# Attention heads: transposes three slots behind their scores, the output projection's first two channel tiles with the fourth pair last, and filling in slots without steps

## The chip, the cores and the metric

The kernel runs on one core of one Trainium2 chip. TensorE (PE) does the matrix products; its weight loads stand in a row of their own (PEld). VectorE (DVE), ScalarE (ACT) and GpSimd (POOL) do the elementwise work, and the queue of SyncE (SP) issues nearly all transfers. The metric is the device time of one execution in microseconds.

## The reference, cut to what matters

Two residual layers over 512 frames of 1024 channels, each followed by a gated MLP. The first layer mixes by pooling, the second by attention with 16 heads of 64 channels. The change lies in the second one alone.

```python
def chunk_attention(h, w_qkv, q_norm, k_norm, rel_table, w_o):
    qkv = h @ w_qkv
    q, k, v = jnp.split(qkv, 3, axis=-1)
    q = head_rmsnorm(q.reshape(B, S, N_HEADS, HEAD_DIM), q_norm)
    k = head_rmsnorm(k.reshape(B, S, N_HEADS, HEAD_DIM), k_norm)
    ...
    def one_chunk(c):          # 64 queries of chunk c, keys of this chunk and the 8 before it
        s = jnp.einsum('bqhd,bkhd->bhqk', qc, kb) * scale + bias[None]
        s = jnp.where(valid[None, None, None, :], s, -1e30)
        p = jax.nn.softmax(s, axis=-1)
        return jnp.einsum('bhqk,bkhd->bqhd', p, vb)
    ...
    return o @ w_o             # added to x
```

## The kernel before

Activations are kept with channels in the partitions: X[0..7] are eight tiles of 128 channels by 512 frames in float32. For accuracy a product is made of three matmuls (`mm3`, L121 to L125: high by high, high by low, low by high part), so every operand is split into a high and a low part (`split`, L94 to L103: ACT or POOL copies the high part, DVE or POOL subtracts it from the raw value for the low part).

`attention` (L917) first projects part of the queries and keys (`project(0)`) and all values, and then runs a loop over 64 **slots** (L1131): slot i holds the steps of tile i, where tile i is head i // 4 and frame block t = i % 4 of 128 frames. A head pair p is two heads, 128 channels. The steps of a slot, in the order in which PE gets them:

- `scores(h, t)` (L1049): two matmuls of up to 512 columns into a PSUM tile `sc`; DVE adds the bias and takes the row's extreme value (L1066), ACT takes the exponential (L1068), DVE the reciprocal (L1069), ACT scales by it (L1070) into the tile `sb`. The biases B of a head are loaded when its first tile comes (L1057, SP's queue).
- `channel_major(p, i)` (L1026) in the third and fourth slot of every eight: four PE transposes of the next pair's queries (i = 0) or keys (i = 1) into a PSUM tile `zt`. For the queries ACT makes the high part `zh` and DVE the low part `zl` (L108); for the keys ACT makes `zh` (L1036) and DVE two half tiles of the low part, `kl` (L1039).
- `turn(h, t)` (L1072): t + 1 PE transposes of `sb` into a PSUM tile `tp`, split by ACT and DVE into `pt..h` and `pt..l` (L102, L103). It comes LAG slots behind the tile's scores.
- `mix(h)` (L1081): eight matmuls, four with the high and four with the low part of the transposed probabilities, into a PSUM tile `oo`, LAGM slots behind the head's last turn; ACT copies one half (`ob`, L1095) and DVE adds the other (`o`, L1096).

When both heads of pair p are mixed, its sum is split into XS[p] and XS[8 + p], halves of the tiles `two` (L1150).

Between the steps `fill` (L1116) puts single matmuls of other products, evenly over the slots: the remaining three projections up to slot 35.5 (matmuls `qk`), then `outputs` (L1022), 144 matmuls `wo` of the output projection from slot 35.5 to slot 64 + FO with FO = LAG + 6. `output(ps_)` (L996) goes through the channel tiles d = 0..7; for each it adds the products with the pairs of `ps_` in a PSUM bank of tag P or Q and lets DVE add the bank to X[d]. `outputs` does this for pairs 0 to 3 and then for 4 and 5. Pairs 6 and 7 follow after the loop (`last_pairs`, L1156).

PE's order is the order in which the code is written (`manual_schedule`, L1113). DVE, ACT, POOL and SP are ordered by a scheduler when the program is built. Each engine works its instructions off in that order. Tiles `sc`, `zt`, `tp` and `oo` share the tag S with four PSUM banks; which of the four a tile gets is settled when the program is built, too, and its first matmul waits until the bank's last tile has been read.

Of the kernel before, what the change touches and what calls it, by code (L numbers as in the profile page):

```python
# [23 lines left out]
P = 128  # L24
S = 512
D = 1024
KD = D // P
# [16 lines left out]
BANKS = {"PQ": 2, "SS": 4}  # L44


LAG, LAGM = 2, 2
FE = (3.5, 19.5, 35.5)
FO = LAG + 6
CM = (2, 3)  # L50
# [22 lines left out]
def trunk(ctx: ExitStack, tc: tile.TileContext, xt, xT, cols, band, edge, poolw, gv, wout, wqk, wv, wo, rel, out):  # L73
    nc = tc.nc
# [7 lines left out]
    X = [act.tile([P, S], F32, name=f"X{k}") for k in range(KD)]  # L82
# [6 lines left out]
    def psum(tag, name, bufs=2):  # L89
        return ps.tile([P, S], F32, name=name, tag=tag, bufs=bufs)  # L90
# [19 lines left out]
    def load_split(src, n, name, pool=None, eng=None, tag=(None, None), eng_hi=None):  # L110

        raw = wp.tile([P, 1024], F32, name=f"{name}_r", tag="wr")
        if pool:
            hi, lo = (pool.tile([P, n], F32R, name=f"{name}_{c}", tag=t, bufs=2 if t == "as" else 1) for c, t in zip("hl", tag))
        else:
            hi, lo = (wp.tile([P, 1024], F32R, name=f"{name}_{c}", tag=f"w{c}", bufs=2) for c in "hl")
        nc.sync.dma_start(raw[:, :n] if len(src.shape) == 2 else raw.rearrange("p (a b) -> p a b", a=src.shape[1]), src)
        split(raw[:, :n], hi[:, :n], lo[:, :n], eng, eng_hi)
        return hi, lo

    def mm3(o, sh, sl, mh, ml, first, last, **how):  # L121

        yield nc.tensor.matmul(o, sh, mh, start=first, stop=False, **how)  # L123
        yield nc.tensor.matmul(o, sh, ml, start=False, stop=False, **how)  # L124
        yield nc.tensor.matmul(o, sl, mh, start=False, stop=last, **how)  # L125

    def run(steps):
        step = None
        for step in steps:
            pass  # L130
        return step
# [9 lines left out]
    def small(name, n, tag="nw"):  # L141
        return tmp.tile([P, n], F32, name=name, tag=f"{tag}{n}", bufs=4)
# [774 lines left out]
    def attention():  # L917
        XS = set2
# [74 lines left out]

            yield from products(ov, wv[half], f"wv{half}", evict=evict)

        def output(ps_, after=None):  # L996

            p0, p1 = ps_[0], ps_[-1] + 1
            n = (p1 - p0) * P
            nd = D // n  # L1000
            w = {}

            def load(d):
                eng = nc.gpsimd if p0 < 6 else None
                w[d] = load_split(wo[d:d + nd, :, p0 * P:p1 * P].rearrange("d p m -> p d m"), D, f"wo{d}_{p0}", eng=eng, eng_hi=eng)

            for d in range(KD):
                if d % nd == 0:
                    if d not in w:
                        load(d)  # L1010
                    hi, lo = w[d]
                o = psum("PQ"[d % 2], f"wo{d}_{p0}")
                for p in ps_:
                    s = slice(d % nd * n + (p - p0) * P, d % nd * n + (p - p0 + 1) * P)
                    yield from mm3(o, hi[:, s], lo[:, s], XS[p], XS[KD + p], p == p0, p == p1 - 1)
                nc.vector.tensor_add(X[d], o, X[d])
                if after:
                    after(d)
                    if d == 1:
                        load(nd)  # L1020

        def outputs():  # L1022
            yield from output(range(4))
            yield from output((4, 5))

        def channel_major(p, i):  # L1026
# [22 lines left out]
        def scores(h, t):  # L1049

            p, e = divmod(h, 2)
            q, k, kl = QK[p, 0][e], QK[p, 1][e], KL[p % 2][e]
            if t == 0:

                base = rdram[h, :]
                for r, n in ((0, S - HD), (HD, S)):
                    nc.sync.dma_start(BT[h % 2][r:r + HD, S - n:], bass.AP(tensor=base.tensor, offset=base.offset + HD, ap=[[1, HD], [1, n]]))  # L1057
            n = (t + 1) * P
            nw = max(n, 256)

            sc = psum("S", f"sc{h}_{t}", 4)
            nc.tensor.matmul(sc[:, :nw], q[:, t * P:n], k[:, :nw], start=True, stop=False)
            nc.tensor.matmul(sc[:, :nw], q[:, t * P:n], kl[:, :nw], start=False, stop=True)  # L1063
            SM[h, t] = s_ = big.tile([P, n], F32, name=f"sb{h}_{t}", tag=f"sb{t}")
            mx = tmp.tile([P, 3], F32, name=f"mx{h}_{t}", tag="mx", bufs=4)
            nc.vector.tensor_tensor_reduce(out=s_[:, :n], in0=sc[:, :n], in1=BT[h % 2][:, :n][:, ::-1], scale=1.0,  # L1066
                                           scalar=3e38, op0=OP.add, op1=OP.min, accum_out=mx[:, 0:1])
            nc.scalar.activation(s_[:, :n], s_[:, :n], AF.Exp, scale=-1.0, bias=mx[:, 0:1], accum_out=mx[:, 1:2])  # L1068
            nc.vector.reciprocal(mx[:, 2:3], mx[:, 1:2])  # L1069
            nc.scalar.activation(s_[:, :n], s_[:, :n], AF.Copy, scale=mx[:, 2:3])  # L1070
# [28 lines left out]
        rcol, r2, late = None, small("r2", TT), []  # L1099
# [13 lines left out]
        with tc.manual_schedule(engines={mybir.EngineType.PE}):  # L1113
            cur, done, kept = 0, 0, 0

            def fill(upto):  # L1116

                nonlocal cur, done
                while cur < len(fillers):
                    g, n, a, b = fillers[cur]  # L1120
                    due = n * (upto - a) / (b - a)
                    while done < min(due, n):
                        next(g)
                        done += 1
                    if upto < b:
                        return
                    run(g)
                    cur, done = cur + 1, 0

            fill(0)  # L1130
            for i in range(nb + LAG + LAGM):  # L1131
                steps = []
                if i < nb:
                    steps.append(lambda: scores(*tiles_[i]))
                if i % 8 in CM and i // 8 + 1 < NPAIR:
                    steps.append(lambda: channel_major(i // 8 + 1, CM.index(i % 8)))
                j = i - LAG
                if 0 <= j < nb:
                    steps.append(lambda: turn(*tiles_[j]))
                j2 = j - LAGM  # L1140
                if 0 <= j2 < nb and j2 % TT == TT - 1:
                    steps.append(lambda: mix(tiles_[j2][0]))
                for x, step in enumerate(steps):
                    step()
                    if late and x < 2:
                        late.pop(0)()
                    fill(i + (x + 1) / len(steps))

                while 8 * kept + 7 <= j2 and (cur == 3 or cur == 2 and done >= 24 * (kept // 2 + 1)):
                    split(O2[kept], XS[kept], XS[KD + kept])  # L1150
                    kept += 1
            fill(nb + FO)
# [37 lines left out]
    with tc.tile_pool(name="ba", bufs=1) as big:  # L1190
        rest = attention()
# [55 lines left out]
```

## Time and profile before

| what | value |
|---|---|
| times of three runs | 972.45, 971.93, 1357.0 us (median 972.45) |
| the profiled execution: its own time | 972.12 us |
| its span in the profile | 970.3 us |
| PE busy, share of the span | 961.6 us, 99% |
| PEld | 815.0 us, 84% |
| DVE | 809.6 us, 83% |
| ACT | 576.6 us, 59% |
| POOL | 102.9 us, 11% |
| PE's share of the chain that ended last | 94% |
| the 64 slots of the loop, first scores to last mix | 452 us to 607 us of the span |

The profiled execution's own time is 1.8 us above its span; the text compares with this execution. A row of the timeline reads: start, duration, engine, line, operation, output tile, input tiles, shapes, and how many instructions are merged in it; in brackets the engine's idle time before it and what ended it. Names leave buffer numbers out: `pt1l` is the low part of the transposed probabilities of odd heads, `two` any XS tile.

### The profile page before, as it was taken

How to read it: one execution, taken by the hardware profiler on the slowest of the kernel's cores; microseconds unless marked ns; L12 is line 12 of the kernel's file. 1: busy time of each engine (PE TensorE's matmuls, PEld its weight loads, DVE VectorE, ACT ScalarE, POOL GpSimd, SP SyncE). 2: the span in 40 equal slices, each digit the busy share in tenths (PEclk: the TensorE clock that was granted, in tenths of full speed). 3: DMA queues.
4: the chain of work that ended last, by engine and by line, in shares of the span. 5: the costliest groups of instructions: out<-in, count | busy, mean ns of one | idle time of the engine just before them, and what ended most of it. 6: DMA issues, size and time to landing. Idle time of an engine off the chain costs nothing.

```text
span 970.3 us, 13704 instructions
## 1 busy us (share of the span) xinstructions
PE 961.6 (99%) x4982; PEld 815.0 (84%) x4982; DVE 809.6 (83%) x1462; ACT 576.6 (59%) x990; POOL 102.9 (11%) x90
## 2 busy tenths in 40 slices
PE   8999999999999999999999999999999999999998
PEld 7788988888888888888888787888988888888886
DVE  8999999999899854442777888999999999989953
ACT  7665564655555544345898988646565565566531
POOL 2300000000000013204534532000000000000000
PEclk9999999999999999999999999999999999999999
DMA  9222332332323224232343341332233233332323
GB/s 342 77 93 71 114 113 75 120 120 92 105 76 120 78 84 147 94 121 91 111 115 107 97 118 55 101 108 80 94 114 104 87 120 108 104 103 77 116 79 109
DMA packets 37427, 102.82 MB, mean 106 GB/s; under 512 B 4432, under 2 KB 7904, under 8 KB 37360
## 3 DMA queue, kind: packets, MB, share of 16 engines
q1 hardware_dynamic: 37296, 101.90, 33.0%
q8 instruction: 39, 0.64, 0.3%
q14 instruction: 28, 0.23, 0.1%
q0 software_dynamic: 32, 0.04, 0.0%
q10 hardware_dynamic: 32, 0.00, 0.0%
HBM read 95.60 MB, written 2.14 MB: 101 GB/s over the span
## 4 chain that ended last, share of the span: by engine, by line
PE 94%; DVE 4%; ACT 2%; issue 0%; DMA 0%; DVEq 0%; ACTq 0%
PE st_m L610 11%; PE out L124 8%; PE out L123 8%; PE out L125 8%; PE st_m L612 6%; PE st_t L610 6%; PE gv L124 4%; PE gv L123 4%; PE gv L125 4%; PE qk L124 3%; PE qk L123 3%; PE qk L125 3%; PE st_t L612 3%; PE st_b L610 3%; PE tp L1078 2%; PE oo L1090 2%
## 5 line engine op out<-in xcount | busy, mean ns | idle before, releaser
L124 PE MATMUL out<-one,ow_h 128*128 128x512 f32 x224 | 87.9, 393 | 0.0
L123 PE MATMUL out<-one,ow_h 128*128 128x512 f32 x224 | 87.8, 392 | 0.0
L125 PE MATMUL out<-one,ow_l 128*128 128x512 f32 x224 | 87.8, 392 | 0.0
L833 DVE TENSOR_TENSOR X<-out,X 128x512 f32<-128x512 f32 (+1 forms) x65 | 44.1, 680 | 49.1 <-PE out L125 48.9
L409 ACT ACTIVATE ow_h<-wo_r 128x640 fp32r<-128x640 f32 (+1 forms) x64 | 50.4, 788 | 56.4 <-PE out L124 46.8
L610 PE MATMUL st_m<-two,g_h 128*128 128x512 f32 x240 | 75.1, 394 | 0.0
L610 PE MATMUL st_m<-h,g_h 128*128 128x512 f32 x240 | 74.0, 389 | 0.0
L410 DVE TENSOR_TENSOR ow_l<-wo_r,ow_h 128x640 fp32r<-128x640 f32 (+1 forms) x64 | 56.5, 883 | 2.5 <-ACT ow_h L409 2.5
L424 DVE SCALAR_TENSOR_TENSOR c<-a,col,c 128x511 f32<-128x511 f32 (+1 forms) x76 | 56.3, 743 | 0.0
L610 PEld LDWEIGHTS st_m<-h,g_h 128*128 128x128 f32 x240 | 45.1, 188 | 10.3
L612 PEld LDWEIGHTS st_m<-two,g_l 128*128 128x128 f32 x240 | 45.0, 188 | 9.5
L610 PEld LDWEIGHTS st_m<-two,g_h 128*128 128x128 f32 x240 | 44.0, 188 | 10.4 <-ACT w L619 0.8
L619 ACT ACTIVATE w<-st_m 128x512 f32<-128x512 f32 x30 | 17.9, 598 | 56.8 <-PE st_m L612 56.8
L125 PE MATMUL qk<-wqk_h,two 128*128 128x512 f32 x128 | 51.4, 402 | 0.0
L123 PE MATMUL qk<-wqk_h,two 128*128 128x512 f32 x128 | 50.8, 409 | 0.0
L124 PE MATMUL qk<-wqk_l,two 128*128 128x512 f32 x128 | 50.8, 397 | 0.0
L612 PE MATMUL st_m<-h,g_l 128*128 128x256 f32 x240 | 48.3, 283 | 0.0
L125 PEld LDWEIGHTS out<-one,ow_l 128*128 128x128 f32 x224 | 42.3, 189 | 6.3
L124 PEld LDWEIGHTS out<-one,ow_h 128*128 128x128 f32 x224 | 42.3, 189 | 6.3 <-DVE one L435 0.3
L612 PE MATMUL st_m<-two,g_l 128*128 128x256 f32 x240 | 47.6, 280 | 0.0
L123 PEld LDWEIGHTS out<-one,ow_h 128*128 128x128 f32 x224 | 42.3, 189 | 6.0
L1066 DVE CUSTOM_DVE_ANT_0 sb<-sc,B 128x128 f32<-128x128 f32 (+1 forms) x64 | 31.1, 486 | 18.9 <-PE sc L1063 18.1
(378 smaller groups left out, 2928.6 us busy)
## 6 DMA issues: line engine op xcount, KB each, us to landing
gv_r<-gv SPq DMA_DIRECT2D x86, 512.0 KB, 3.9
wo_r<-wout SPq DMA_DIRECT2D x32, 384.0 KB, 3.1
wo_r<-wout SPq DMA_DIRECT2D x32, 320.0 KB, 2.9
wqk_r<-wqk SPq DMA_DIRECT2D x16, 512.0 KB, 3.4
wv_r<-wv SPq DMA_DIRECT2D x8, 512.0 KB, 3.3
wo_r<-wo SPq DMA_DIRECT2D x8, 512.0 KB, 3.4
xt<-xt SPq DMA_DIRECT2D x4, 512.0 KB, 5.1
X<-xT SPq DMA_DIRECT2D x8, 256.0 KB, 7.4
```

The lines of the kernel that those rows point to most:

```text
L123: yield nc.tensor.matmul(o, sh, mh, start=first, stop=False, **how)
L124: yield nc.tensor.matmul(o, sh, ml, start=False, stop=False, **how)
L125: yield nc.tensor.matmul(o, sl, mh, start=False, stop=last, **how)
L409: nc.scalar.activation(hi[:, :n], raw[:, :n], AF.Copy)
L410: return hi, lo, lambda: nc.vector.tensor_sub(lo[:, :n], raw[:, :n], hi[:, :n].bitcast(F32))
L424: nc.vector.scalar_tensor_tensor(c[:, j:], a[:, :S - j], cw[2 - j], c[:, j:], op0=OP.mult, op1=OP.add)
L610: nc.tensor.matmul(o, hi[:, c], B[i, name], start=first and i == 0, stop=False, **how)
L612: nc.tensor.matmul(o[:, 0], lo[:, c], B[i, name][:, 0], start=False, stop=i == 3, **how)
L833: nc.vector.tensor_add(X[d][:, fs], o[:, fs], X[d][:, fs])
L1066: nc.vector.tensor_tensor_reduce(out=s_[:, :n], in0=sc[:, :n], in1=BT[h % 2][:, :n][:, ::-1], scale=1.0, scalar=3e38, op0=OP.add, op1=OP.m ...
L1078: nc.tensor.transpose(tp[:, j * P:(j + 1) * P], s_[:, j * P:(j + 1) * P], ident)
L1090: nc.tensor.matmul(oo[:, j * P:], V[j, h // 4][:, h % 4].rearrange("p a d -> p (a d)"), PT[e][c][:, 4 * j:3 * j + TT].rearrange("p t q -> ...
```

## The change

There are three edits in `attention`, and no instruction is added or removed on any engine.

1. LAG goes from 2 to 3: the turn of a tile comes one slot later, and with it the mix (LAGM stays 2). FO follows, so that the 144 fill matmuls of the output projection are spread to slot 73 instead of 72.
2. `output` gets an argument `late`. With late=2, which the call for pairs 0 to 3 uses, channel tiles 0 and 1 first take pairs 0, 1 and 2 each, and then pair 3 for the one and for the other; their banks in P and Q stay open together for that time.
3. A `fill(i + 1)` stands behind the steps of each slot. It issues something only in a slot without steps, which is slot 67, between the last turn (slot 66) and the last mix (slot 68).

```diff
-LAG, LAGM = 2, 2
+LAG, LAGM = 3, 2
...
-        def output(ps_, after=None):
+        def output(ps_, after=None, late=0):
...
+            o = {}
+
+            def product(d, p):
+                if d not in o:
+                    o[d] = psum("PQ"[d % 2], f"wo{d}_{p0}")
+                hi, lo = w[d // nd * nd]
+                s = slice(d % nd * n + (p - p0) * P, d % nd * n + (p - p0 + 1) * P)
+                yield from mm3(o[d], hi[:, s], lo[:, s], XS[p], XS[KD + p], p == p0, p == p1 - 1)
+
             for d in range(KD):
-                if d % nd == 0:
-                    if d not in w:
-                        load(d)
-                    hi, lo = w[d]
-                o = psum("PQ"[d % 2], f"wo{d}_{p0}")
+                if d % nd == 0 and d not in w:
+                    load(d)
+                if d < late:
+                    for p in ps_[:-1]:
+                        yield from product(d, p)
+                    if d + 1 < late:
+                        continue
+                    for e in range(late):
+                        yield from product(e, ps_[-1])
+                        nc.vector.tensor_add(X[e], o[e], X[e])
+                    continue
                 for p in ps_:
-                    s = slice(d % nd * n + (p - p0) * P, d % nd * n + (p - p0 + 1) * P)
-                    yield from mm3(o, hi[:, s], lo[:, s], XS[p], XS[KD + p], p == p0, p == p1 - 1)
-                nc.vector.tensor_add(X[d], o, X[d])
+                    yield from product(d, p)
+                nc.vector.tensor_add(X[d], o[d], X[d])
...
-            yield from output(range(4))
+            yield from output(range(4), late=2)
             yield from output((4, 5))
...
                     fill(i + (x + 1) / len(steps))
+                fill(i + 1)
```

What this does to the order of the engines is shown at three places. In the rows, a tile's name has its number in it: sc11_0 is head 11, block 0; oo9 head 9; zt6_1 the keys of pair 6; wo0_0 channel tile 0 of the call for pairs 0 to 3; two1 and two5 hold the high and low parts of pairs 2 and 3.

**PE around the mix of head 9.** Before, from the last of the key transposes of pair 6 to the mix:

```order
L1032 MATMUL zt6_1_5591<-ident_106,z3_3_5366 128x128
L124 MATMUL wo2_0_5548<-two5_101,wo2_0_h_5543 128x512
L1078 MATMUL tp10_1_5605<-ident_106,sb10_1_5526 128x128 x2
L125 MATMUL wo2_0_5548<-two1_97,wo2_0_l_5544 128x512
L1090 MATMUL oo9_5611<-pt1h_3627,one2_82 128x512
```

And now:

```order
L1046 MATMUL zt6_1_5587<-ident_106,z3_3_5362 128x128
L124 MATMUL wo2_0_5541<-two5_101,wo2_0_h_5536 128x512
L1092 MATMUL tp10_0_5601<-ident_106,sb10_0_5488 128x128
L125 MATMUL wo2_0_5541<-two1_97,wo2_0_l_5537 128x512
L1076 MATMUL sc11_0_5608<-z25_1_5355,z25_0_5315 128x256
L1077 MATMUL sc11_0_5608<-kl11_3632,z25_0_5315 128x256
L123 MATMUL wo2_0_5541<-two1_97,wo2_0_h_5536 128x512
L1092 MATMUL tp10_1_5618<-ident_106,sb10_1_5520 128x128 x2
L124 MATMUL wo2_0_5541<-two5_101,wo2_0_h_5536 128x512
L125 MATMUL wo2_0_5541<-two1_97,wo2_0_l_5537 128x512
L1104 MATMUL oo9_5625<-pt1h_3627,one2_82 128x512
```

The mix moved from the slot of the key transposes into the next slot, behind another turn and the next head's first scores. Its bank is another one as well: before, oo9 followed zt6_0 (the queries of pair 6) in its bank; now it follows zt6_1 (the keys). The same holds for oo11 with pair 7, and oo3 now follows the keys of pair 3; oo7 now follows sc9_0, the scores of its own slot.

**DVE at the same place.** Before:

```order
L1066 ISA sb10_3_5584,mx10_3_5585<-sc10_3_5581,B0_3637 128x512
L1066 ISA mx10_3_5585 128x1
L108 SCALAR_TENSOR_TENSOR zl6_0_5568<-zt6_0_5561,gq_109,zh6_0_5566 128x512
L103 TENSOR_TENSOR pt0l_3626<-tp10_0_5576,pt0h_3625 128x128
L1039 SCALAR_TENSOR_TENSOR kl00_3629<-zt6_1_5591,gq_109,zh6_1_5596 64x512
L1039 SCALAR_TENSOR_TENSOR kl01_3630<-zt6_1_5591,gq_109,zh6_1_5596 64x512
```

And now:

```order
L108 SCALAR_TENSOR_TENSOR zl6_0_5561<-zt6_0_5554,gq_109,zh6_0_5559 128x512
L1080 ISA sb10_3_5579,mx10_3_5580<-sc10_3_5576,B0_3637 128x512
L1080 ISA mx10_3_5580 128x1
L103 TENSOR_TENSOR pt1l_3628<-tp9_3_5568,pt1h_3627 128x4x128
L1053 SCALAR_TENSOR_TENSOR kl00_3629<-zt6_1_5587,gq_109,zh6_1_5592 64x512
L1053 SCALAR_TENSOR_TENSOR kl01_3630<-zt6_1_5587,gq_109,zh6_1_5592 64x512
L1080 ISA sb11_0_5611,mx11_0_5612<-sc11_0_5608,B1_3638 128x128
```

The low part of the queries now stands ahead of the scores of block 3, and the low part of head 9's last turn ahead of the two `kl`.

**PE at the first use of the fourth pair.** Before, in channel tile 0 (the last L125 of pair 2, then pair 3 from the second row on):

```order
L125 MATMUL wo0_0_5379<-two1_97,wo0_0_l_5375 128x512
L123 MATMUL wo0_0_5379<-two1_97,wo0_0_h_5374 128x512
L1062 MATMUL sc9_2_5452<-z24_1_5110,z24_0_5078 128x384
L1063 MATMUL sc9_2_5452<-kl01_3630,z24_0_5078 128x384
L124 MATMUL wo0_0_5379<-two5_101,wo0_0_h_5374 128x512
```

And now, behind the products of channel tile 1 with pair 2:

```order
L125 MATMUL wo1_0_5444<-two1_97,wo0_0_l_5366 128x512
L1076 MATMUL sc10_0_5485<-zh5_1_5354,zh5_0_5314 128x256
L1077 MATMUL sc10_0_5485<-kl10_3631,zh5_0_5314 128x256
L123 MATMUL wo0_0_5370<-two1_97,wo0_0_h_5365 128x512
L1092 MATMUL tp9_1_5495<-ident_106,sb9_1_5429 128x128 x2
L124 MATMUL wo0_0_5370<-two5_101,wo0_0_h_5365 128x512
```

Pair 3 is asked for nine matmuls of the filling later than before, among the scores of head 10 instead of those of head 9.

On SP's queue the loads of the biases of heads 10 and 11 changed places with their neighbours: those of head 11 now stand behind the first transfer of the queries of pair 6, and those of head 13 between the transfers of pair 7. POOL's order is the same as before.

## The prediction

> **What bounds the kernel now.** First the page: the span, the busy shares and the chain that ended last.
>
> ```profile
> span 970.3 us, 13704 instructions
> PE 961.6 (99%) x4982; PEld 815.0 (84%) x4982; DVE 809.6 (83%) x1462; ACT 576.6 (59%) x990; POOL 102.9 (11%) x90
> PE 94%; DVE 4%; ACT 2%; issue 0%; DMA 0%; DVEq 0%; ACTq 0%
> ```
>
> PE is the bound over the whole span. The change neither adds nor removes a matmul, so it can win only time in which PE stands still inside the loop, and lose by new waits there. The next view cuts the loop into windows; its columns are window, length and then the busy time of PE, PEld, DVE, ACT and POOL, the granted clock, the DMA share and GB/s.
>
> ```profile
> 452.00:544.00 92.00, 92.00 (x503) 77.62 (x502) 63.92 (x192) 79.32 (x189) 40.02 (x29) 1.00 0.37 109
> 544.00:553.00 9.00, 8.08 (x42) 5.87 (x42) 8.65 (x29) 7.55 (x23) 3.10 (x3) 1.00 0.45 129
> 553.00:585.00 32.00, 31.96 (x186) 26.75 (x186) 27.22 (x82) 28.45 (x76) 17.30 (x14) 1.00 0.37 98
> 585.00:600.00 15.00, 14.81 (x84) 12.11 (x83) 11.92 (x37) 13.06 (x35) 3.44 (x2) 1.00 0.29 87
> 600.00:607.00 7.00, 6.19 (x35) 4.95 (x34) 4.97 (x11) 5.06 (x9) 0.00 (x0) 1.00 0.01 2
> ```
>
> The clock is 1.00 throughout. PE is idle in none of the first 92 us (the projections fill them), and for 0.92 + 0.04 + 0.19 + 0.81 = 1.96 us behind. That undercounts, because a matmul's row is longer than its turn. The distance of two starts shows the turn:
>
> ```profile
> 602.96 0.60 PE L1078 MATMUL tp<-ident,sb 128*128 128x128 f32 x4
> 603.32 0.47 PE L123 MATMUL wo<-two,wo_h 128*128 128x512 f32 x1
> 603.63 0.39 PE L124 MATMUL wo<-two,wo_h 128*128 128x512 f32 x1
> 603.85 0.39 PE L125 MATMUL wo<-two,wo_l 128*128 128x512 f32 x1
> ```
>
> A matmul of 512 columns has a row of 0.39 but the next starts 0.22 to 0.23 behind it; four transposes take 0.36, and the matmul behind transposes 0.31. A distance above these is a wait, even where the rows touch. By starts I find the following waits between 544 and 607 us.
>
> The Trainium skill, "Perfetto Trace Analysis", section "Identifying the Most-Contended Engine", says that the matmul's busy share is no good measure of the room left, since pipelined matmuls look different in a trace from what they cost. The trace agrees here: by busy rows 1.96 us could be won at most, by starts about twice that.
>
> **What the change removes.** (a) The waits for the fourth pair, XS[3]:
>
> ```profile
> 547.58 0.48 PE L125 MATMUL wo<-two,wo_l 128*128 128x512 f32 x1
> 548.10 0.50 PE L123 MATMUL wo<-two,wo_h 128*128 128x512 f32 x1
> 548.43 0.33 PE L1062 MATMUL sc<-z,z 128*128 128x384 f32 x1
> 548.60 0.34 PE L1063 MATMUL sc<-kl,z 128*128 128x384 f32 x1
> 549.61 0.49 PE L124 MATMUL wo<-two,wo_h 128*128 128x512 f32 x1 [0.66 <-DVE two L103]
> 549.94 0.39 PE L125 MATMUL wo<-two,wo_l 128*128 128x512 f32 x1
> ```
>
> L123 needs the high part and comes 0.52 behind (0.32 would do behind four transposes): 0.2. L124 needs the low part and comes 1.01 behind a score of 384 columns, whose turn is 0.17 to 0.18: 0.83. The start-up behind such a stop costs about 0.1, twice (0.33 for 0.23): together **1.2 us**. In the changed order nine more fill matmuls, 9 x 0.23 = 2.1 us, stand ahead of the first use, and in the program 13 matmuls, four pairs of scores and three turns lie between mix(7) and it: 3.0 + 1.3 + 0.9 = 5.2 us for the high part, 5.55 for the low one.
>
> ```profile
> 543.78 0.81 PE L1090 MATMUL oo<-pt1l,one 128*128 128x512 f32 x4
> 544.43 0.45 PE L124 MATMUL wo<-two,wo_h 128*128 128x512 f32 x1
> 548.87 0.68 DVE L103 TENSOR_TENSOR two<-o,two 128x512 fp32r<-128x512 f32 x1
> ```
>
> Before, the mix ended at 544.43 and the low part at 549.55, 5.1 us behind; that is in time by 0.4, so what is late next here is little. Two banks stay open longer, but no other matmul of the filling asks for P or Q in that time.
>
> (b) Waits of a turn for its scaled probabilities, the first and the last of seven:
>
> ```profile
> 545.19 0.40 PE L123 MATMUL wo<-two,wo_h 128*128 128x512 f32 x1
> 545.70 0.52 PE L1078 MATMUL tp<-ident,sb 128*128 128x128 f32 x3
> 600.93 0.44 PE L124 MATMUL wo<-two,wo_h 128*128 128x512 f32 x1
> 601.65 0.55 PE L1078 MATMUL tp<-ident,sb 128*128 128x128 f32 x3 [0.28 <-ACT sb L1070]
> ```
>
> 0.51 for 0.23 is 0.28; 0.72 for 0.23 is 0.49; the seven (0.13 to 0.49) sum to **1.8 us**. A slot later means 155 us / 64 = 2.4 us later, five times the largest of them. Nothing is queued behind the turn that waits for less.
>
> (c) The last mix, whose low part comes late:
>
> ```profile
> 604.32 0.78 PE L1090 MATMUL oo<-pt1h,one 128*128 128x512 f32 x4
> 605.63 0.87 PE L1090 MATMUL oo<-pt1l,one 128*128 128x512 f32 x4 [0.53 <-DVE pt1l L103]
> 606.33 0.45 PE L124 MATMUL wo<-two,wo_h 128*128 128x512 f32 x1
> ```
>
> 1.31 between the halves where 0.65 is usual (543.78 to 544.43): **0.65 us**. The filling in slot 67 puts seven matmuls between the last turn and this mix in place of four, 0.7 us more, which just covers it. The price on the other side: the work behind the mix. Its sum is split by
>
> ```profile
> 608.55 0.69 DVE L103 TENSOR_TENSOR two<-o,two 128x512 fp32r<-128x512 f32 x1
> ```
>
> that is, at 609.24, 2.9 us behind the mix's end. 22 fill matmuls (5 us) still follow the mix, so this stays covered.
>
> (d) Mixes of heads 9 and 11, which before waited for the bank of the queries, zt_0:
>
> ```profile
> 559.57 0.60 PE L1032 MATMUL zt<-ident,z 128*128 128x128 f32 x4
> 560.38 0.41 PE L1078 MATMUL tp<-ident,sb 128*128 128x128 f32 x2
> 560.54 0.47 PE L125 MATMUL wo<-two,wo_l 128*128 128x512 f32 x1
> 561.04 0.82 PE L1090 MATMUL oo<-pt1h,one 128*128 128x512 f32 x4
> 560.14 0.75 DVE L108 SCALAR_TENSOR_TENSOR zl<-zt,gq,zh 128x512 f32<-128x512 f32 x1
> 561.00 1.50 DVE L1039 SCALAR_TENSOR_TENSOR kl<-zt,gq,zh 64x512 fp32r<-64x512 f32 x2
> ```
>
> oo9 starts 0.50 behind L125 where 0.31 would do: 0.18, and as much at oo11, **0.36**. It starts 0.15 behind zl's end (560.89), which gives the delay from a reader's end to the bank's next matmul. Removed in all: 1.2 + 1.8 + 0.65 + 0.36 = **about 4.1 us**.
>
> **What it adds.** The order of banks is new: oo9 and oo11 now follow the keys, which are read until the second kl ends. From the start of zt to kl's end took 562.50 - 559.57 = 2.93 here, 3.08 with the 0.15. In the new order lie between zt's first transpose and the mix: zt 0.35, five fill matmuls (three behind transposes at 0.31, two at 0.23), one pair of scores of 256 columns 0.23 (half the columns, twice) and turns of one and two blocks, 0.05 and 0.16 (the latter from 560.38 to 560.54, the former an estimate below it), together 0.35 + 0.31 + 0.05 + 0.31 + 0.23 + 0.23 + 0.16 + 0.31 + 0.23 = 2.18. So 3.08 - 2.18 = 0.9 of new wait at each. The other instance of kl in the trace bounds it above:
>
> ```profile
> 542.08 0.60 PE L1032 MATMUL zt<-ident,z 128*128 128x128 f32 x4
> 544.71 0.28 PE L1062 MATMUL sc<-z,z 128*128 128x256 f32 x1
> 544.05 1.50 DVE L1039 SCALAR_TENSOR_TENSOR kl<-zt,gq,zh 64x512 fp32r<-64x512 f32 x2
> 546.13 0.28 DVE L1066 CUSTOM_DVE_ANT_0 sb<-sc,B 128x128 f32<-128x128 f32 x1
> ```
>
> 545.55 - 542.08 = 3.47, with 0.15 a wait of 1.44. Below it is 0, if DVE and ACT are early. I take 0.9, the row of the very place. oo3 follows the keys of pair 3 with 3.10 between: 0 to 0.52, I take 0.3. oo7 follows sc9_0: its reduction ended 1.70 behind the scores' start, with 1.16 between and the 0.15 that is 0.69; there the reduction stood behind kl, so half, 0.35. What waits behind a mix is the whole of PE, so each counts in full. The scores' biases of heads 11 and 13 are loaded behind one or more transfers on SP's queue now:
>
> ```profile
> B<-rdram SPq DMA_DIRECT2D x16, 128.0 KB, 3.1
> ```
>
> 3.1 us against slots of 2.4 us: for this and smaller shifts 0.2 (0 to 0.5). Added: 0.9 + 0.9 + 0.3 + 0.35 + 0.2 = **2.65 us**, bounds 0 and 4.6.
>
> The Trainium skill, "Perfetto Trace Analysis", section "Matmuls", says that independent groups of matmuls should rotate through PSUM banks so that ACT and DVE empty one under the next group's matmuls. By that rule four banks in turn would hide these readings and the added term would be 0, which the rivals weigh; oo9's 0.50 shows that four banks don't hide them all even before.
>
> **Sum.** -4.1 + 2.65 = -1.45 against the profiled execution's own 972.12 us (0.33 below the median of the runs shown): **970.7 us**. Since 2% is 19 us, about what a measurement of this kernel can tell from no change, the call is no change.
>
> **The rivals.**
> 1. *All waits go and none comes.* The readings are done under the matmuls: 972.12 - 4.1 = 968.0. For it: DVE has 4.8 us free in the 32 us from 553 on. Against it: oo9's bank wait of 0.18 in the trace, with a shorter reading than kl. Chance 0.2.
> 2. *Slower: DVE's queue makes kl late.* DVE now has the low part of a turn of four blocks (0.69, as in the rows of 608.55 and 548.87) ahead of kl at oo9 where it had one block. If kl starts one such instruction (0.6) later at oo3, oo7, oo9 and oo11, the added waits are 2.65 + 4 x 0.6 = 5.05, and the time 972.12 + 0.95 = 973.1. It turns slower than before once those four waits exceed 4.1 less 0.2, that is, if kl is over 0.35 late on the mean. For it: DVE busy 8.65 of 9 us and 27.22 of 32. Against it: kl started at 561.00, with ACT's high part and not with DVE. Chance 0.15.
> 3. *The waits for the scaled probabilities stay.* They are ACT's (28.45 busy of 32, 13.06 of 15); if ACT does them a slot later too, because its order is built anew, 1.8 doesn't come back: 972.12 - 2.3 + 2.65 = 972.5. Against it: 2.4 us is far more than a wait of 0.5. Chance 0.2. That would also be the case of a change that does nothing.
>
> **How the numbers follow.** My forecast has 0.45, for 969.8 to 971.6. The range of 8 in 10 reaches from rival 1 to most of rival 2: 968.3 to 972.9, leaving about 0.08 below and 0.1 above. All cases lie within 19 us, so within 2% gets 0.98, and 0.01 stays for each side, for an order of which I have overlooked something large.
>
> **What would show it.** Right: no wait of L124 on two at the first use of pair 3; no wait of tp on sb over 0.1; the two halves of oo15 at 0.65; oo9 and oo11 starting about 0.15 behind kl's end, with 1.1 to 1.3 us behind the matmul ahead of them in place of 0.50. Wrong: if oo9 and oo11 start at 0.23 to 0.31 behind it (rival 1), if tp waits stay near 1.8 (rival 3), or if kl's end lies over 3.4 us behind zt's start (rival 2). A wait at a place that I have not followed, for example scores on biases, would make the sum wrong.

## The result, and the profile after

The changed kernel is slower: 974.5 us against 972.12 us (medians of 13 runs each), a ratio of 1.0023 with a 95% interval of 1.0014 to 1.0032. That is above the predicted 970.7 and above the range's end at 972.9. One of the 13 runs of before took 1357 us; what slowed it is not known, and it is outside the ratio. The difference is small, 0.23%, but clear of the spread of the runs. The profiled execution of the changed kernel took 973.87 us, with a span of 972.1.

From the page after:

```profile
span 972.1 us, 13684 instructions
PE 961.8 (99%) x4982; PEld 815.4 (84%) x4982; DVE 812.5 (84%) x1462; ACT 575.7 (59%) x990; POOL 102.2 (11%) x90
```

PE's busy time is the same within 0.2 us (961.6 before); the span is 1.8 us longer, and nearly all of that is PE standing still. The windows after, with the columns of before (window, length, busy PE, PEld, DVE, ACT, POOL, clock, DMA share, GB/s):

```profile
452.00:544.00 92.00, 91.40 (x499) 76.85 (x498) 64.03 (x190) 77.88 (x186) 39.89 (x29) 1.00 0.36 108
544.00:553.00 9.00, 8.84 (x49) 7.11 (x49) 8.83 (x30) 8.68 (x25) 3.14 (x3) 1.00 0.27 79
553.00:585.00 32.00, 29.88 (x171) 24.52 (x171) 26.05 (x79) 27.61 (x71) 15.36 (x14) 1.00 0.43 114
585.00:600.00 15.00, 14.05 (x81) 11.62 (x80) 12.58 (x38) 12.08 (x35) 4.83 (x3) 1.00 0.19 57
600.00:607.00 7.00, 7.00 (x39) 5.86 (x38) 5.79 (x15) 5.66 (x13) 0.00 (x0) 1.00 0.20 69
```

The first of the two places that were emptied, 544 to 553, has 0.16 us idle in place of 0.92, and the end, 600 to 607, 0 in place of 0.81. But the middle, which before had 0.04 idle in 32 us, now has 2.12, 585 to 600 has 0.95 in place of 0.19, and even the first 92 us, full before, have 0.60. PE's longest waits in the loop, from the view of waits after (who waits, for whom, total, times, longest):

```profile
PE oo L1104 <- DVE kl L1053: 2.1, 3, 0.8
PE tp L1092 <- DVE pt0l L103: 0.9, 1, 0.9
PE zt L1046 <- POOL z L979: 0.6, 1, 0.6
```

None of these three lines existed before; the lines of the three waits that did (the filling for `two`, the turns for `sb`, the last mix for `pt1l`) are gone. By distances of starts, as in the prediction, the loop's waits are:

| wait of PE in the loop, us | before | after |
|---|---|---|
| filling for the fourth pair, with start-up | 1.23 | 0 |
| turns for scaled probabilities | 1.80 | 0 |
| last mix for its low part, with start-up | 0.80 | 0 |
| mixes 9 and 11 on their bank | 0.36 | 0.90 + 0.94 |
| mix 3 on its bank (keys of pair 3) | 0 | 0.77 |
| mixes 7, 8 and 12 | 0 | 0.32 + 0.07 + 0.19 |
| query transposes of pair 6, for POOL | 0 | 0.77 |
| turn of head 13, block 1, behind a low part on DVE | 0 | 1.08 |
| scores and turns around 577 us | 0 | 0.47 |
| filling for a low part of weights, 619.6 us | 0 | 0.25 |
| turn at 544.6 | 0 | 0.12 |
| sum | 4.19 | 5.88 |

The difference, 1.7 us, is nearly all of the 1.75 by which the loop is longer. I measure the loop from the first scores' start to the last `wo` matmul's start, since the loop begins between 452.2 and 453.9 us in the profiles below, while from the last `wo` matmul's start to the end of the span it is 348.0 to 348.1 us in all of them. Here are the two ends, before and after:

```profile
452.47 0.28 PE L1062 MATMUL sc<-zh,zh 128*128 128x256 f32 x1
622.29 0.39 PE L125 MATMUL wo<-two,wo_l 128*128 128x512 f32 x1
452.46 0.28 PE L1076 MATMUL sc<-zh,zh 128*128 128x256 f32 x1
624.03 0.39 PE L125 MATMUL wo<-two,wo_l 128*128 128x512 f32 x1
```

169.82 us before, 171.57 after. What went away is best seen at pair 3's first use and at the last mix, in PE's rows after:

```profile
551.99 0.40 PE L123 MATMUL wo<-two,wo_h 128*128 128x512 f32 x1
552.22 0.38 PE L1092 MATMUL tp<-ident,sb 128*128 128x128 f32 x2
552.36 0.48 PE L124 MATMUL wo<-two,wo_h 128*128 128x512 f32 x1
607.48 0.74 PE L1104 MATMUL oo<-pt1h,one 128*128 128x512 f32 x4
608.05 0.81 PE L1104 MATMUL oo<-pt1l,one 128*128 128x512 f32 x4
```

0.23 and 0.14 between the first three, the plain turns, and 0.57 between the halves of the last mix (1.31 before). What came is mainly three different things. **First, banks.** PE and DVE around the mix of head 9, and around that of head 3:

```profile
559.71 0.60 PE L1046 MATMUL zt<-ident,z 128*128 128x128 f32 x4
561.12 1.51 DVE L1053 SCALAR_TENSOR_TENSOR kl<-zt,gq,zh 64x512 fp32r<-64x512 f32 x2 [0.36 <-ACT zh L1050]
561.65 0.40 PE L125 MATMUL wo<-two,wo_l 128*128 128x512 f32 x1
562.78 0.82 PE L1104 MATMUL oo<-pt1h,one 128*128 128x512 f32 x4 [0.73 <-DVE kl L1053]
503.06 0.60 PE L1046 MATMUL zt<-ident,z 128*128 128x128 f32 x4
505.27 1.50 DVE L1053 SCALAR_TENSOR_TENSOR kl<-zt,gq,zh 64x512 fp32r<-64x512 f32 x2
505.92 0.40 PE L124 MATMUL qk<-wqk_l,two 128*128 128x512 f32 x1
506.92 0.76 PE L1104 MATMUL oo<-pt1h,one 128*128 128x512 f32 x3 [0.60 <-DVE kl L1053]
```

Both mixes start 0.15 behind kl's end (562.63 and 506.77). At head 9 kl ends 2.92 behind the keys' first transpose, at head 3 3.71. Head 11 differs from head 9. Its rows on DVE after, and those of the same kl and of head 3's kl before:

```profile
577.26 0.68 DVE L103 TENSOR_TENSOR pt1l<-tp,pt1h 128x512 fp32r<-128x512 f32 x1
577.86 1.51 DVE L1053 SCALAR_TENSOR_TENSOR kl<-zt,gq,zh 64x512 fp32r<-64x512 f32 x2
577.08 1.50 DVE L1039 SCALAR_TENSOR_TENSOR kl<-zt,gq,zh 64x512 fp32r<-64x512 f32 x2
505.38 1.50 DVE L1039 SCALAR_TENSOR_TENSOR kl<-zt,gq,zh 64x512 fp32r<-64x512 f32 x2
```

At head 11 the keys' transposes start at 575.88, so kl ends 3.48 behind them, against 2.95 before (575.63 to 578.58): the low part of a turn of four blocks now stands ahead of it in DVE's queue, 0.6 behind the end of ACT's high part (577.25). At head 3 it was 3.58 before (from 503.30).

**Second, a tile that isn't ready.** POOL scales the projected queries block by block (L979); PE's transposes of pair 6 stop ahead of the last one:

```profile
553.62 4.05 POOL L979 TENSOR_TENSOR z<-z,qk_y 128x512 f32<-128x512 f32 x4 [6.27 <-DVE mx L1083]
556.62 0.49 PE L1046 MATMUL zt<-ident,z 128*128 128x128 f32 x3
557.72 0.33 PE L1046 MATMUL zt<-ident,z 128*128 128x128 f32 x1 [0.60 <-POOL z L979]
```

and before:

```profile
553.05 4.05 POOL L979 TENSOR_TENSOR z<-z,qk_y 128x512 f32<-128x512 f32 x4 [5.81 <-DVE qk_y L977]
```

POOL ends 0.57 later than before, because DVE's factor `qk_y` comes that much later, and PE, without its waits for the fourth pair, is here 1.0 us earlier (557.62 before). Before, the last block was ready 0.8 us ahead of its transpose; 0.57 + 1.0 less that is about the 0.77 that PE now waits.

**Third, DVE held up by POOL.** Rows of PE, DVE and POOL after, and the same two subtractions before:

```profile
583.98 2.40 POOL L103 TENSOR_TENSOR wo_l<-wo_r,wo_h 128x1024 fp32r<-128x1024 f32 x1
584.69 2.24 DVE L103 TENSOR_TENSOR two<-o,two 128x512 fp32r<-128x512 f32 x1
586.86 0.68 DVE L103 TENSOR_TENSOR pt0l<-tp,pt0h 128x512 fp32r<-128x512 f32 x1
587.59 0.44 PE L1092 MATMUL tp<-ident,sb 128*128 128x128 f32 x2 [0.92 <-DVE pt0l L103]
582.04 0.68 DVE L103 TENSOR_TENSOR two<-o,two 128x512 fp32r<-128x512 f32 x1
582.07 2.93 POOL L103 TENSOR_TENSOR wo_l<-wo_r,wo_h 128x1024 fp32r<-128x1024 f32 x1
```

The low part of pair 5 on DVE took 2.24 us in place of 0.68, because POOL's subtraction had begun 0.71 earlier: POOL ends at 586.38 and DVE 0.55 later. Before, DVE began 0.03 ahead of POOL, and it was POOL's row that was stretched, from 2.40 to 2.93. The subtraction from PSUM that stands behind it in DVE's queue came late, and the turn that waits for its bank with it. The Trainium skill, "SBUF — State Buffer", section "Who interferes with whom", says that DVE and GpSimd contend for one shared pair of ports, as an exclusive lock, and that a DVE instruction with two SBUF inputs contends with a GpSimd instruction that reads SBUF. These rows agree: both inputs of `two` are in SBUF, and each engine waits out the other's whole instruction. I call this the lock below.

### The profile page after: what moved, and what is told of

It is laid out like the page before. It is cut to its first block, busy times and chain, and to the rows that moved or that the text cites. A ratio compares the mean times of both kernels' runs of the same rounds, so it can differ in the third digit from the quotient of the medians.

```text
span 972.1 us, 13684 instructions
## 1 busy us (share of the span) xinstructions
PE 961.8 (99%) x4982; PEld 815.4 (84%) x4982; DVE 812.5 (84%) x1462; ACT 575.7 (59%) x990; POOL 102.2 (11%) x90
## 5 line engine op out<-in xcount | busy, mean ns | idle before, releaser
L125 PE MATMUL out<-one,ow_l 128*128 128x512 f32 x224 | 87.8, 392 | 0.0
L125 PE MATMUL qk<-wqk_h,two 128*128 128x512 f32 x128 | 51.5, 402 | 0.0
L125 PEld LDWEIGHTS out<-one,ow_l 128*128 128x128 f32 x224 | 42.3, 189 | 6.3
```

## The experiments

All kernels stand beside the kernel before on the same chip, in five rounds; the ratio is to before. "Loop" is the length defined above, from the one profiled execution of each. One execution has its own scatter: the 12 runs of before that count lie within 0.9 us (971.87 to 972.74), those of the change within 1.9 (973.81 to 975.75). I therefore don't read anything into a difference of loops under about half a microsecond.

| kernel | median us | ratio to before, 95% | loop us |
|---|---|---|---|
| before | 972.1 | 1 | 169.82 |
| the change | 974.5 | 1.0023 [1.0014, 1.0032] | 171.57 |
| late_alone | 972.28 | 1.0001 [0.9992, 1.0009] | 169.88 |
| fill_alone | 971.76 | 0.9995 [0.9987, 1.0004] | 169.35 |
| lag_alone | 975.91 | 1.0043 [1.0030, 1.0057] | 173.25 |
| late_fill | 971.46 | 0.9991 [0.9983, 1.0000] | 168.83 |
| keys_fifth_slot | 973.48 | 1.0015 [1.0006, 1.0023] | 171.13 |
| pool_quarters | 972.64 | 1.0004 [0.9995, 1.0012] | 170.21 |
| keys_fifth_quarters | 971.64 | 0.9994 [0.9986, 1.0003] | 169.05 |
| later_keys_quarters | 989.56 | 1.0177 [1.0159, 1.0195] | 186.13 |
| projection_earlier | 973.78 | 1.0020 [1.0011, 1.0028] | 171.53 |
| mix_before_turn | 970.65 | 0.9986 [0.9978, 0.9995] | 168.22 |
| mix_first_quarters | 971.27 | 0.9993 [0.9984, 1.0002] | 168.92 |
| mix_first_quarters_fe | 970.78 | 0.9991 [0.9982, 1.0000] | 168.24 |
| mix_first_dve_block | 969.79 | 0.9973 [0.9964, 0.9982] | 167.43 |
| mix_first_slots_4_5 | 975.80 | 1.0038 [1.0024, 1.0052] | 172.83 |

### Each edit by itself

**late_alone**: `LAG, LAGM = 2, 2` and no `fill(i + 1)`; `output(range(4), late=2)` stays.

> The second edit alone on the kernel before (LAG 2, no filling behind the steps). Theory 1 (the terms removed were right, and a wait that goes is partly given back where the next tile isn't ready): the 1.2 us of waits for the fourth pair go, but the query transposes of pair 6 then come 1.2 us earlier, while POOL finished their last block only 0.8 us before they needed it: 0.4 is given back there, -0.8 us against before. Theory 2 (the waits for the fourth pair were worth nothing, since they only hid later ones): 0 against before.

The loop is 0.06 us longer. The waits for the fourth pair went as expected, but not where theory 1 put the loss: the turns of head 9 took it, waiting for their scaled probabilities (PE's rows in this kernel):

```profile
552.07 0.40 PE L123 MATMUL wo<-two,wo_h 128*128 128x512 f32 x1
553.29 0.44 PE L1092 MATMUL tp<-ident,sb 128*128 128x128 f32 x2 [0.82 <-ACT sb L1084]
```

1.22 between the two, 0.99 too much, and another turn 0.42, where before that stretch had 0.25 behind the waits for pair 3. Against that, the 0.34 at the mix of head 9 and the turn ahead of it is gone. What makes the loop come out even is a wait of 0.45 of the scores at 571.40, for which the profile shows no cause and which late_fill, with the same edit, does not have. So the fourth pair's wait was mostly cover for ACT and DVE: of the 1.2 us, about 0.4 is won by itself, and the runs' interval cannot tell that from nothing.

**fill_alone**: `LAG, LAGM = 2, 2` and `output(range(4))`; `fill(i + 1)` stays.

> The third edit alone on the kernel before. Theory 1: the matmuls in the slot without steps cover the wait of the last mix for its low part: -0.65 us against before, nothing else moves. Theory 2 (the wait goes to the next step): 0.

The loop is 0.47 shorter: the last mix's 0.80 is gone, and 0.25 came back at 617 us, where the filling now meets the low part of the last weights (`wo_l`) before DVE has made it. The run's interval takes in 1.

**lag_alone**: the first edit only.

> The first edit alone (LAG 3 and FO 9, pair 3 not late, no filling in the empty slot). Theory 1: mix 7 comes a slot (2.4 us) later against the same place of the filling, so the wait for the fourth pair grows from 1.2 to some 3.6; turns win 1.8 and mixes 9 and 11 their 0.36; bank waits behind the keys (0.77 + 0.90 + 0.94) and the turn behind the low part of pair 5 (1.08) come in, the last mix still waits 0.65: about +3.5 to +4.5 us against before. Theory 2 (LAG alone brings the loss of the whole change and the two others nothing): +2.4.

+3.4 in the loop, near the 3.5 to 4.5 of theory 1. The wait for the fourth pair grows to 2.1 only, not to some 3.6. The large new waits of the changed kernel are there (banks 0.77, 0.90, 0.94; the turn of head 13 1.10), all but the transposes' wait for POOL, because PE stands ahead of it for pair 3:

```profile
550.55 0.50 PE L123 MATMUL wo<-two,wo_h 128*128 128x512 f32 x1 [1.70 <-ACT two L102]
```

**late_fill**: the change with `LAG, LAGM = 2, 2`.

> The second and third edits without the first (LAG back to 2, FO 8). Theory 1 (the loss is LAG's, and the others add what they did alone, in the loop's length +0.06 and -0.47): -0.4 us against before, about 971.7; the turns' waits for the scaled probabilities (1.8 before, more with the second edit) stay. Theory 2 (the edits' gains are independent and were masked by other differences): -1.9, about 970.2.

-0.99 in the loop and -0.75 in the medians, about twice theory 1's sum and half of theory 2's. Without the 0.45 at 571.40 in late_alone the two single gains add up to 0.86, near this one. The turns wait 2.8 us here. Against this kernel LAG 3 removes these 2.8 and 0.18 at mix 11, and brings 5.6 of the 5.88: the loss of the change is LAG's, and it is 2.7 us in the loop.

### The banks

**keys_fifth_slot**: on the changed kernel,

```diff
-CM = (2, 3)
+CM = (2, 4)
```

> The changed kernel with the key transposes one slot later (CM from (2, 3) to (2, 4)), the queries unmoved. By the program's order no mix then follows keys in its bank. Theory 1 (the mixes of heads 3, 9 and 11 wait 0.77, 0.90 and 0.94 for the keys' low part to leave the bank): these three go, and head 7's 0.3: -2.6 to -2.9 us against the changed kernel, so about 0.5 us under before; the waits of the query transposes of pair 6 for POOL (0.77) and of the turn of head 13 (1.08) stay. Theory 2 (the mixes wait because DVE is behind as a whole, and the bank is only where it shows): the waits turn up at other places and the time stays within 0.7 us of the changed kernel.

Only 0.44 in the loop and 1.0 in the medians, nearer to theory 2 in size. The four mixes' waits went, 2.9 us, but nearly as much came: turns behind the keys in their banks (0.48, 0.26, 0.38), and this (rows of POOL, DVE and PE of this kernel):

```profile
546.83 2.38 POOL L103 TENSOR_TENSOR wo_l<-wo_r,wo_h 128x1024 fp32r<-128x1024 f32 x1
547.79 1.48 DVE L974 TENSOR_TENSOR qk_a<-qk_s,r 128x32 f32<-128x32 f32 x1
549.77 0.44 PE L1076 MATMUL sc<-z,z 128*128 128x384 f32 x1 [0.97 <-DVE pt0l L103]
```

A product of 32 columns, 0.17 us elsewhere, took 1.48 until POOL was done (549.21), and scores waited 1.13 for what stood behind it. This is the lock between DVE and POOL, at another place, and not a DVE that is behind as a whole; keys_fifth_quarters below separates the two.

**mix_before_turn**: in a slot that has both, the mix is put ahead of the turn.

```diff
-                if 0 <= j < nb:
-                    steps.append(lambda: turn(*tiles_[j]))
                 j2 = j - LAGM
                 if 0 <= j2 < nb and j2 % TT == TT - 1:
                     steps.append(lambda: mix(tiles_[j2][0]))
+                if 0 <= j < nb:
+                    steps.append(lambda: turn(*tiles_[j]))
```

> The changed kernel with the mix ahead of the turn in the slots that have both; keys and queries stay in their slots. By the program's order a mix then takes the bank of the scores of the slot before, and the turn behind it the bank of the keys, 1.3 us of mix later. Theory 1 (the three mixes wait for the keys' low part in their bank): these waits (0.77 + 0.90 + 0.94, and 0.3 of head 7) go, the turns behind them wait at most 0.2 to 0.4 for the keys: -1.8 to -2.6 us against the changed kernel, 972 to 972.7. Theory 2 (waits only move): within 0.7 us of the changed kernel, as other waits take their place.

-3.4 in the loop and -3.9 in the medians against the change, more than theory 1's upper end, and under the kernel before (0.14%, interval 0.05 to 0.22). PE and DVE around the mix of head 9 here:

```profile
561.28 0.39 PE L123 MATMUL wo<-two,wo_h 128*128 128x512 f32 x1
561.52 0.75 PE L1104 MATMUL oo<-pt1h,one 128*128 128x512 f32 x4
561.44 1.52 DVE L1053 SCALAR_TENSOR_TENSOR kl<-zt,gq,zh 64x512 fp32r<-64x512 f32 x2 [0.19 <-ACT zh L1050]
563.26 0.38 PE L1092 MATMUL tp<-ident,sb 128*128 128x128 f32 x2
```

The mix starts 0.24 behind the matmul ahead of it, while kl is only beginning, and the turn behind the mix comes 0.30 after kl's end: the keys' bank is emptied under the mix. The gain is not the banks' 2.93 alone: the lock's 1.08 is gone too, because the low part of pair 5 happens to start ahead of POOL's subtraction here (0.83 us), and so is the 0.47 around 577 us, while the query transposes of pair 4 now wait 0.16 + 0.89 for POOL. The Trainium skill, "Perfetto Trace Analysis", section "Matmuls", asks for banks in rotation so that their emptying hides under the next group; the runs agree where the step behind the keys is long enough, and the change showed that four banks in turn don't do it by themselves.

### The lock between DVE and POOL

**pool_quarters**: on the changed kernel, in `split`,

```diff
+        if eng is nc.gpsimd:
+            for c in range(0, 1024, 256):
+                step = eng.tensor_sub(lo[:, c:c + 256], raw[:, c:c + 256], hi[:, c:c + 256].bitcast(F32))
+            return step
```

> The changed kernel with POOL's subtraction for a low part (128 x 1024, 2.4 us) cut into four of 256 columns; all else as it is. In the changed kernel the low part of pair 5 on DVE took 2.24 us in place of 0.68, up to half a microsecond behind the end of POOL's subtraction, and the turn of head 13, block 1, waited 1.08 us behind it. Theory 1 (a DVE subtraction of two SBUF operands cannot run while POOL's runs, and waits for the end of that instruction): it now waits for a quarter, at most 0.6 us, its row is at most 1.3 us, and the turn's wait falls to 0.2 or less: -0.9 to -1.1 us. Theory 2 (the row is long because its own operand came late): the row stays at 2.2 and the time within 0.3 us.

-1.36 in the loop; DVE's and POOL's rows:

```profile
585.00 0.87 DVE L107 TENSOR_TENSOR two<-o,two 128x512 fp32r<-128x512 f32 x1
584.59 3.29 POOL L105 TENSOR_TENSOR wo_l<-wo_r,wo_h 128x256 fp32r<-128x256 f32 x4
545.26 2.83 POOL L105 TENSOR_TENSOR wo_l<-wo_r,wo_h 128x256 fp32r<-128x256 f32 x4
```

DVE's low part again starts behind POOL's subtraction, by 0.41, but takes 0.87 in place of 2.24: it gets in between two quarters. The turn's wait is gone, and mix 12's 0.19 behind it. Theory 1 holds, and the ratio's interval lies below that of the change. The price is POOL's: 2.83 us, in the last row, for what takes 2.40 in one piece (3.29 where DVE gets in between).

**keys_fifth_quarters**: both edits.

> Keys one slot later and POOL's subtraction in quarters, on the changed kernel. With the keys alone, the mixes' waits went, but two waits behind DVE's low parts stood there (1.13 at 549.8 us and 1.18 at 587.5 us), both behind a DVE instruction that was stretched (0.17 to 1.48, 0.68 to 1.98) while POOL's subtraction ran. Theory 1 (these two are the lock between DVE and POOL): both go, -1.8 to -2.2 us against the keys alone, about 971.4. Theory 2 (DVE is behind as a whole and the waits move on): less than 0.7 us is won.

-2.1 in the loop against the keys alone: of the two waits of 1.13 and 1.18, 0.17 and 0.20 are left.

**mix_first_quarters**: the mix ahead of the turn, and the quarters.

> The same with POOL's subtraction in quarters. Theory 1 (bank and lock are separate causes, worth 1.08 for the lock in the changed kernel): another -1.0 to -1.4 us against the mix ahead of the turn alone, about 971. Theory 2: less than 0.5.

A miss: +0.7 in the loop and +0.6 in the medians. There was no wait behind the lock left to remove, and POOL's slower subtraction delays its scaling: the query transposes of pair 4 wait 0.63 + 0.89 us for POOL instead of 0.16 + 0.89.

### The unready queries

**projection_earlier**: the changed kernel with `FE = (3.5, 19.5, 35.0)`, and **mix_first_quarters_fe**: the same on mix_first_quarters.

> The changed kernel with the projections' end half a slot earlier alone (FE 35.0). Theory 1 (the query transposes of pair 6 wait 0.77 us for POOL because the waits for the fourth pair that held PE up ahead of them are gone): the wait goes, -0.5 to -0.8 us against the changed kernel, about 973.8. Theory 2: the wait turns up at the mix of head 9 or later, 0.

The wait for POOL falls from 0.77 to 0.41 and the loop by 0.04 only, the medians by 0.7. A turn now waits 0.83 at 549.6 behind another product stretched by the lock (0.17 to 1.35), and mix 5 0.49 for its bank. The orders of all engines were built anew, so this run does not tell the theories apart.

> The same again with the projections' end half a slot earlier (FE from (3.5, 19.5, 35.5) to (3.5, 19.5, 35.0)). Theory 1: POOL has scaled the last block of pair 6 about 1.2 us earlier and the query transposes' wait of 0.77 goes: -0.5 to -0.8 us, about 970.4, the best of all. Theory 2 (that wait is given back at the next unready tile, since DVE or ACT run late there): 0 to +0.5.

-0.7 in the loop against mix_first_quarters and -0.5 in the medians, but the two ratios are 0.9991 and 0.9993 with intervals that nearly coincide, so the gain isn't shown. Nor would it be by theory 1's mechanism: at pair 6 the waits for POOL rise from 0.74 to 0.15 + 0.89. The waits at pair 4 are the ones that went.

**later_keys_quarters**: `CM = (4, 5)` and the quarters on the changed kernel.

> The changed kernel with queries and keys three and two slots later (CM from (2, 3) to (4, 5)) and POOL's subtraction in quarters. By the program's order no mix follows keys in its bank, and the queries of pair 6 come 4.8 us later, behind POOL's scaling. Theory 1 (three separate causes: banks 2.9, lock 1.1, unready projection 0.77): all go, -4 to -4.8 us against the changed kernel, 969.7 to 970.5, under both kernels. Theory 2 (waits only move, since ACT and DVE are nearly full there): 971.5 to 973.

The largest miss: +17 us against the kernel before. The halves of the keys are moved by SP's queue, and there they now stand behind a load of biases that waits for DVE; the scores wait four times, 13.2 us in all, for that transfer. What a longer stop costs besides shows in the windows around one of them (columns as above):

```profile
553.20:559.00 5.80, 0.51 (x3) 0.07 (x1) 2.92 (x12) 2.45 (x6) 2.67 (x3) 0.82 0.47 152
559.00:564.00 5.00, 4.92 (x17) 4.33 (x18) 0.96 (x5) 1.76 (x5) 1.37 (x2) 0.53 0.00 0
564.00:570.00 6.00, 6.00 (x37) 5.13 (x36) 5.18 (x17) 4.40 (x14) 3.88 (x5) 1.00 0.02 5
```

**mix_first_dve_block**: on mix_before_turn,

```diff
-                    nc.gpsimd.tensor_mul(Z[c, t], Z[c, t], ...)
+                    (nc.vector if t == 3 else nc.gpsimd).tensor_mul(Z[c, t], Z[c, t], ...)
```

> The mix ahead of the turn, and of each projection's four blocks that POOL scales one after the other (1.0 us each) the last one is scaled by DVE. In the kernel with the mix ahead of the turn the query transposes still wait 0.16 + 0.89 + 0.75 us for POOL's blocks of pairs 4 and 6. Theory 1 (an unready block is a cost of its own, and PE is in front of POOL because earlier waits are gone): about 1.0 of the 1.8 us goes, 969.6 to 970.0, if DVE's block takes 0.7 us beside POOL. Theory 2 (DVE's product of two SBUF operands queues behind POOL's, which holds the lock): the block comes as late as before and DVE's queue is held up behind it, 0 to +2 us.

-0.8 in the loop and -0.9 in the medians against mix_before_turn: theory 1 for the size, and the lowest time of all, 0.27% under the kernel before (interval 0.18 to 0.36, which overlaps that of mix_before_turn at its edge). The two engines' rows at pair 6:

```profile
553.50 0.69 DVE L979 TENSOR_TENSOR z<-z,qk_y 128x512 f32<-128x512 f32 x1
553.54 3.56 POOL L979 TENSOR_TENSOR z<-z,qk_y 128x512 f32<-128x512 f32 x3 [6.17 <-DVE qk_y L977]
```

DVE got the lock 0.04 earlier; POOL's three blocks take 3.56, half a microsecond more than three quarters of 4.05, and are still done 0.9 earlier than four (557.10 against 557.98). The waits at pair 6 fall from 0.75 to 0.37, at pair 4 from 1.05 to 0.61.

**mix_first_slots_4_5**: on mix_before_turn, `CM = (3, 4)`.

> The mix ahead of the turn, with queries and keys one slot later each (CM (3, 4)). Theory 1 (unready blocks cost the 1.8 us by themselves): the queries come 2.4 us later, these waits go, and new bank waits behind scores are 0.3 to 0.8: -1.0 to -1.5 us against the mix ahead of the turn, 969.2 to 969.7. Theory 2 (the transfers of the keys now come too late, as with slots 5 and 6, where they cost 17 us, or the wait is given back to another): 970.6 or more.

Theory 2, and worse: +4.6 in the loop. No transpose waits for POOL any more, but scores, turns and mixes behind new neighbours in their banks do (1.31, 1.03, 0.88, 0.63, 0.58), where 0.3 to 0.8 was expected.

## Why the prediction was wrong

- **What the change removes: right.** 4.1 us predicted, 4.19 counted, and each of the four terms is gone in the trace after.
- **Mix 9: right.** 0.9 predicted, 0.90 measured, with the start 0.15 behind kl's end, kl's end 2.92 behind the transposes (2.93 predicted) and the mix 1.13 behind the matmul ahead, as "1.1 to 1.3" had it.
- **Mixes 11 and 7: right in size, in part by luck.** 0.9 and 0.35 predicted, 0.94 and 0.32 measured. At head 11 DVE's queue made kl 0.53 later than before, as rival 2 had it; by the prediction's own sum that is a wait of 3.48 + 0.15 - 2.18 = 1.45. But PE had lost 0.47 just ahead of it, around 577 us, so that 0.94 was left. At mix 7 the bank was the cause, as predicted: the scores' reduction ended at 545.28, 0.15 ahead of the mix. The 0.35, though, was half of 0.69 for want of a better number.
- **Mix 3: mis-sized**, 0.3 for 0.77. The distance in the program was right (3.09 from the rows, 3.10 predicted), but kl ended 3.71 behind the transposes. The bound of 3.47 came from "the other instance of kl in the trace", and that was an oversight: the loop before has seven, and the one of this very place took 3.58, from which the same sum gives 0.64 (3.58 + 0.15 - 3.09). The new order added only 0.13.
- **The step that failed** is the last term of the sum, "for this and smaller shifts 0.2 (0 to 0.5)". It measured 2.9 us: 1.08 behind the lock, 0.77 for POOL's block, 0.47 around 577 us, 0.25 at 619 us, 0.26 at mixes 8 and 12, 0.12 at a turn. None of it was a wait for biases, the cause that the term was built on. With 0.9 + 0.94 + 0.77 + 0.32 + 2.9 in place of 2.65 the sum gives +1.7. All that was added, 5.88, is also over the stated bound of 4.6.
- **"What is late next here is little" also failed.** I looked for what was late next at the same tile only. PE comes 1.0 us earlier to the next places, and there POOL's scaling, itself 0.57 later, had only 0.8 us to spare. late_alone shows the same: 1.2 us removed, about 0.4 won.
- **The rivals**: the sign is that of rival 2, and its condition (the four bank waits over 3.9 us) was not met: they sum to 2.93. Its mechanism did show at head 11, and "kl's end over 3.4 us behind zt's start" was met at heads 11 and 3 (3.48 and 3.71), not at head 9 (2.92). The change came out slower by two mechanisms that no rival had, together 1.85 us: the lock, which was readable before in the stretched 2.93 of POOL's row, and the unready block, whose slack of 0.8 us stood in the trace of before. Rival 3 fell: no turn waits for `sb` any more.

What stays open: how much of the 0.47 around 577 us is DVE's order and how much the banks; nothing was run for it alone. And the later slots show waits that I can name but not forecast.

## What to carry to other kernels

On an engine that is full, a removed wait is only worth what the next late thing leaves of it: follow the engine past the place, and list every tile that it will now reach earlier with the slack that it had. When steps are moved past each other, list who owned each shared buffer before, and put the longest step behind the slowest reader; here swapping mix and turn won 3.4 us in the loop, more than the 1.75 that the whole change cost, though part of it came from the lock, which went by a chance of the new order. And look for instructions that ran beside each other on DVE and POOL: which started first was here decided by 0.03 and 0.04 us, and the loser's queue paid for the rest of the other's instruction.

## What the runs showed of the hardware

- A DVE operation with two SBUF operands and a POOL subtraction or product excluded each other for a whole instruction, in either direction: DVE 0.68 to 2.24 and 0.17 to 1.48, POOL 2.40 to 2.93. A DVE subtraction with an operand in PSUM was not stretched: of 128 x 384 at 584.22 in the changed kernel, under the same POOL subtraction (583.98 to 586.38) that held up `two`, it took 0.55, as elsewhere. At pair 4 of mix_first_dve_block DVE came 0.33 behind a POOL subtraction, and its block took 2.62 in place of 0.69.
- In later_keys_quarters PE stood still for 5.4 us, from 553.71 to 559.08. In windows of one microsecond its granted clock was 1.00 up to 556, 0.96 from 556 to 557 and 0.50 from there on, so it fell some 3.2 us into the stop; over the first 5 us of work it was 0.53 on the mean, and 1.00 from 564 on. The waits of around 1 us, and one of 1.70 in lag_alone, left it at 1.00. The Trainium skill, "TensorE: Matmul & The Clock Gate", section "HAM oscillation — how this bites in real kernels", warns of idle gaps over some 3.4 us; the trace agrees with both, 5.4 and about 1.
- Cutting a 128 x 1024 subtraction on POOL in four cost 0.43 us (2.40 to 2.83). From the subtraction's start to that of POOL's next instruction, at pair 4, it is much the same: 2.37 in mix_before_turn, 2.81 in mix_first_quarters.
